# A hybrid scan/attention layer on one Trainium2 core: the scan's queue order around three kinds of short copies

## The chip, the cores and the metric

The kernel runs on one core of one Trainium2 chip. The metric is the device time of one execution in microseconds (us); the time before is the median of three runs. The core has five engines that each work through a queue of their own in order: TensorE (PE in the profile; its weight loads are listed apart as PEld), VectorE (DVE), ScalarE (ACT), GpSimd (POOL) and SyncE (SP). In this kernel SP does nothing but issue DMA transfers, and every transfer is issued there.

## The reference, cut to what matters

One layer of a streaming encoder on 1088 tokens: 1024 of a new prompt and 64 that continue a running stream, with 1024 features. All is fp32.

```
proj = rmsnorm(x) @ w_in          # z | xBC | dt | q | k | v | gate_ssm | gate_att
xs, B, C = silu(causal_conv(xBC)) # 4 groups, each 512 rows of xs and 128 rows of B and of C
per group, over chunks of tokens:
  y      = ((C B^T) * decay) @ (dt * xs) + exp(acum) * (C @ state)
  state  = decay_end * state + B^T @ (to_end * dt * xs)
y_ssm = rmsnorm_per_group((y + D * xs) * silu(z)) * w
o     = diff_attention(q, k, v)
mix   = sigmoid(gate_ssm) * (y_ssm @ w_branch_ssm) + sigmoid(gate_att) * (o @ w_branch_attn)
x    += mix @ w_out
x    += conv_ffn(rmsnorm(x))
```

The prompt starts a group with an empty state; the 64 sample tokens start from a given one. The features of `y_ssm` are 2048, twice those of `o`.

## The kernel before, in words

**Layout.** Activations lie feature by token: 128 features on the partitions, tokens along the row. The 1088 tokens are cut into three column spans `WIDE` of 384, 384 and 320. A large matrix product is made in three terms: each fp32 operand is cast to a rounded type (`hi`) and the difference is kept (`lo`), and `product` (L155 to L160) adds hi*hi, hi*lo and lo*hi over eight slices of 128, 24 matmuls into one bank of PSUM. `acc` (L118) hands the banks out in rotation; in the scan's stage three banks serve, two named `mm` and one named `mx`.

**Order.** The program is traced in Python from top to bottom, and each instruction has the place at which it was traced as its priority. A scheduling pass then writes out one fixed order for each engine. `tc.high_priority(n)` moves what its block traces ahead by n places. `tc.issue_after(ins)` puts what its block traces on the engine of `ins` behind `ins` in that engine's queue; it does not wait for the end of `ins`, and it binds no other engine. What an instruction reads and writes is guarded by semaphores: an instruction at the head of its queue waits for its inputs, and all behind it in that queue wait with it. A tile pool with `bufs=n` has n buffers for a name; the n+1st use waits until the first is no longer read.

**Stages.** Input projections and attention come first, then the scan with what is woven into it, then a third branch product, the output projection and the FFN. The gates are projected by `gate_tiles` (L525), woven into attention and scan, and stored to `g_sc` in DRAM (L533); the branch product reads them from there.

**The scan** (`scan`, L917) goes over 4 groups, each with the three spans, each cut into steps of 128 tokens (the last step of a group has 64): nine steps a group, 36 in all, counted here from 0. Span number `i` runs from 0 to 11, so `i == 6` is the first span of the third group, steps 18, 19 and 20 (`o` = 0, P, 2P). A step has two parts.

- `front` (L826), begun one step ahead: ScalarE makes the exponentials `e2` (L833), TensorE transposes the rows (`tr`, L836) and B (L838) and multiplies B and C into `cb` (L839); ScalarE copies `cb` to `b_cb` (L841); VectorE makes `xx` (L845); GpSimd masks the decay rows `bc` (L846), ScalarE takes their exponentials (L848), VectorE multiplies them by `b_cb` (L849).
- `back` (L852): TensorE makes `yi` (L857) and, with a state, `ye` (L863), which VectorE combines into `y` (L864, L865); at a group's first step there is no state, and ScalarE copies `yi` (L867). TensorE makes the new contribution `stp` (L869). At a group's first step ScalarE copies it to `state` (L872); later GpSimd decays the old state (L874) and VectorE adds (L876). The banks `tr`, `cb`, `yi`, `ye` and `stp` are one each.

At the end of a span follow, in this order:

- `gated` (L881), at the span's last step: VectorE adds D * xs (L883, four), GpSimd multiplies by the gate rows `zin` (L884), ScalarE squares (L885), GpSimd adds the squares in two steps (L886, L887);
- `normed` (L889), in the second step of the next span: TensorE sums over the partitions (`gst`, L891), ScalarE copies to `grs` (L894), and `rstd_of` makes the root;
- `scaled` (L898), in the third step of the next span: VectorE multiplies by the root (L901, four). For groups 0 and 1 ScalarE casts to the hi half in two pieces (L909), written over `zin`, VectorE makes the differences over `y` (L910), and two DMAs store the halves to `y_sc` (L913); for groups 2 and 3 one DMA stores `y` (L904).

The read of the gate rows of the span after (`fetch_z`, L814, `zin`, two buffers) stands behind `scaled` at L952; the rows of a span (`fetch`, L807, buffer `in`, two) are asked for at L959, and the decay rows `bc` (`ask`, L819, four buffers) three steps ahead. The buffers of `y` are two as well (L945).

**What is woven in.** `scan` yields in each step and once more behind a span's `gated`, and at each yield `fill(1.5)` (L593, L986) takes pieces of other work: first the rest of the gate, z and conv projections, then from span `BRANCH_AT` = 4 on the branch products (`branch_tiles`, L974). A piece is one `product` of `branch` (L171): one 128-row block of the output by one span of columns. `branch` asks for its input rows (L178, two calls for each half and span: 12 DMAs), then goes over `TURNS` (L46): the first turn has blocks 0 and 1, so pieces 0 to 5 are (block, span) = (0,0), (1,0), (0,1), (1,1), (0,2), (1,2). For each piece it asks for the gate rows beside it (L192, `b_g`, eight buffers), multiplies, and VectorE empties the bank with the gate, (tanh + 1) * product (L203); a DMA stores the result. The first `branch`, on the attention's `o_sc` with the gates `g_sc[D:]`, is the one that begins in the scan's span 4 (L979); the second (L980) has no gates; the third, after the scan (L1008), has gates and two rows to add.

Of the kernel before, what the change touches and what calls it, by code (L numbers as in the profile page):

```python
# [17 lines left out]
P = 128  # L18
# [45 lines left out]
BRANCH_AT = 4  # L64

# [15 lines left out]
def hybrid_layer(ctx: ExitStack, tc: tile.TileContext, xT, xt, prm, cst, rope, wvd, win, wbs, wba, wout, wup, wdn,  # L81
# [73 lines left out]
    def product(ps, terms):  # L155
        n = len(terms)
        for i, (a_hi, a_lo, b_hi, b_lo) in enumerate(terms):
            PE.matmul(ps, a_hi, b_hi, start=i == 0, stop=False)  # L158
            PE.matmul(ps, a_hi, b_lo, start=False, stop=False)  # L159
            PE.matmul(ps, a_lo, b_hi, start=False, stop=i == n - 1)  # L160
# [9 lines left out]

    def branch(stage, side, src, wts, gates, adds, out, step=1):  # L171

        parts = rows_by_part("b")
        for (c, w), (hi, lo) in zip(WIDE, parts):
            for k in range(0, KT, step):
                if stage is None:
                    for u, t in enumerate((hi, lo)):
                        load(out=t[:, k : k + step].bitcast(F32),  # L178
                             in_=src[D * u + P * k : D * u + P * (k + step), c : c + w].rearrange("(k p) t -> p k t", p=P))
                else:  # L180
                    t = stage()[:, :w]
                    load(out=t, in_=src[P * k : P * (k + 1), c : c + w])
                    S.copy(hi[:, k], t)
                    V.tensor_tensor(out=lo[:, k], in0=t, in1=hi[:, k], op=ALU.subtract)
        for ms in TURNS:
            wt = [weights(wts[m], KT, P) for m in ms]
            for (c, w), (hi, lo) in zip(WIDE, parts):
                for m, (w_hi, w_lo) in zip(ms, wt):
                    beside = []
                    for d, r0 in ([(g_sc, gates)] if gates is not None else []) + [(d, 0) for d in adds]:  # L190
                        t = side()[:, :w]
                        load(out=t, in_=d[r0 + P * m : r0 + P * (m + 1), c : c + w])  # L192
                        beside.append(t)
# [4 lines left out]
                    product(ps, [(w_hi[:, k], w_lo[:, k], hi[:, k], lo[:, k]) for k in range(KT)])  # L198
# [605 lines left out]
    with (tc.tile_pool(name="sin", bufs=1) as sin, tc.tile_pool(name="sp", bufs=1) as sp,  # L804
# [21 lines left out]
        def front(g, ch, o, bx, xs, bc):  # L826
# [14 lines left out]
            S.copy(b_cb[:L, : P + L], cb[:L, : P + L])  # L841
# [10 lines left out]
        def back(g, ch, bx, y, state, start, L, cs, bc, e2, b_cb, xdt, xw):  # L852
# [18 lines left out]
            if state is None:  # L871
                S.copy(new, up)  # L872
            else:
                G.tensor_tensor(out=new.rearrange("p (e q) -> p e q", e=8), in0=state.rearrange("p (e q) -> p e q", e=8),  # L874
                                in1=decs[:, ch, h8].unsqueeze(2).to_broadcast([P, 8, 64]), op=ALU.mult)
                V.tensor_tensor(out=new, in0=new, in1=up, op=ALU.add)  # L876
# [4 lines left out]
        def gated(g, c, w, xs, zt, y):  # L881
            for j in range(4):
                V.scalar_tensor_tensor(y[:, j], xs[:, j, :w], col(O_D + 4 * g + j), y[:, j], ALU.mult, ALU.add)  # L883
            G.tensor_tensor(out=y, in0=y, in1=zt, op=ALU.mult)  # L884
            act(zt, y, AF.Square)  # L885
# [12 lines left out]
        def scaled(g, c, w, xs, zt, y, rs):  # L898
# [3 lines left out]
            if g >= 2:  # L902
                r0 = D * 2 + 4 * P * (g - 2)
                load(out=y_sc[r0 : r0 + 4 * P, c : c + w].rearrange("(j p) t -> p j t", p=P), in_=y)  # L904
                return
# [11 lines left out]
        def scan():  # L917
# [14 lines left out]
            coming = begin(0)  # L932
            for n, (i, g, c, w, o) in enumerate(steps):
                now, coming = coming, begin(n + 1)
# [11 lines left out]
                state = back(g, (c + o) // P, bx, y, state, start, *now)  # L946
                if o == 1 * P and due is not None:
                    rs = normed(*due)
                if o == 2 * P and due is not None:
                    scaled(*due, rs)  # L950
                    if i + 1 < len(spans):
                        gates.append(fetch_z(*spans[i + 1]))  # L952
                if c + o + P >= min(c + w, T):
# [3 lines left out]
                    gated(*due)  # L957
                    if i + 2 < len(spans):
                        got.append(fetch(*spans[i + 2]))  # L959
                    yield i  # L960
            with tc.high_priority(LAST):
                gated(*due)
                scaled(*due, normed(*due))
                for d, t in ends:
# [483 lines left out]
```

## Time and profile before

| | us |
|---|---|
| median of three runs | 2463.59 |
| lowest and highest of them | 2461.98, 2466.84 |
| the profiled execution, as timed | 2464.61 |
| span of its trace | 2462.8 |
| TensorE in the stretch 1050 to 1550 (end of attention, scan): busy | 492.99 of 500 |
| VectorE, ScalarE, GpSimd in the same stretch: busy | 321.74, 267.17, 158.22 |
| DMA share there, and GB/s | 0.69, 236 |
| mean granted TensorE clock there | 0.99 |

Times within the trace count from the start of the span. In rows of a timeline the columns are the start, the duration, the engine, the source line, the operation with out<-in tiles and sizes, and in brackets how long the engine sat idle before it and what ended that. A DMA's row on SP (SPq) is the issue of it, not the transfer. In a table of stretches each engine has its busy time and its count of instructions; a clock of 0.50 is a TensorE that the throttle granted half its rate.

### The profile page before, as it was taken

The numbers are of one execution on the slowest core, as the hardware profiler recorded it, in microseconds if no ns is written. First come the engines' busy times: TensorE is split into PE (matmuls) and PEld (weight loads), VectorE is DVE, ScalarE is ACT, GpSimd is POOL, SyncE is SP. The second block draws the span as 40 slices with busy tenths as digits, with TensorE's granted clock in tenths as the row PEclk, the third lists the DMA queues.
The fourth block names the chain that finished last, engine by engine and source line by source line (L and its number), as shares of the span: only waits on it lengthen the run. The fifth ranks groups of instructions, "written<-read, shape, count | busy, mean of one in ns | idle before, by whom it ended". The sixth has DMA issues, their size and how long they took to land.

```text
span 2462.8 us, 42894 instructions
## 1 busy us (share of the span) xinstructions
PE 2439.4 (99%) x16560; PEld 2363.9 (96%) x16560; DVE 1517.6 (62%) x2574; ACT 1110.8 (45%) x2389; POOL 471.4 (19%) x532
## 2 busy tenths in 40 slices
PE   8999999999999999999999999999999999999999
PEld 8999999999999999998889999999999999999999
DVE  4356266745877577538776664656976677672422
ACT  6244344645665466446664453434544333351200
POOL 0000000100111000005432341012255555530000
PEclk9999999999999999999999999999999999999999
DMA  7237277543444353255697864664222222265542
GB/s 253 91 109 260 93 277 220 160 148 104 151 146 137 119 166 112 89 188 183 227 352 240 304 210 155 221 207 138 68 84 80 80 74 73 79 231 196 188 156 90
DMA packets 221678, 397.61 MB, mean 161 GB/s; under 512 B 31065, under 2 KB 147042, under 8 KB 221346
## 3 DMA queue, kind: packets, MB, share of 16 engines
q1 hardware_dynamic: 221474, 394.88, 48.2%
q8 instruction: 130, 2.13, 0.4%
q14 instruction: 74, 0.61, 0.1%
HBM read 269.03 MB, written 125.76 MB: 160 GB/s over the span
## 4 chain that ended last, share of the span: by engine, by line
PE 88%; DVE 4%; DMA 3%; ACT 1%; issue 1%; POOL 1%; SPq 0%; POOLq 0%; DVEq 0%; ACTq 0%
PE mm L158 13%; PE mm L160 13%; PE mm L159 13%; PE mx L1220 12%; PE mx L160 6%; PE mx L159 6%; PE mx L158 6%; PE mm L1220 5%; PE po L726 3%; PE sc L679 2%; PE sc L678 2%; PE pt L707 1%; PE ye L863 1%; PE yi L857 1%; PE stp L869 1%
## 5 line engine op out<-in xcount | busy, mean ns | idle before, releaser
L158 PE MATMUL mm<-xn_hi,w_hi 128*128 128x384 f32 (+1 forms) x1408 | 471.2, 335 | 1.1 <-DVE zr L542 0.9
L160 PE MATMUL mm<-xn_hi,w_lo 128*128 128x384 f32 (+1 forms) x1408 | 467.8, 332 | 0.5 <-DVE w_lo L152 0.5
L159 PE MATMUL mm<-xn_lo,w_hi 128*128 128x384 f32 (+1 forms) x1408 | 467.1, 332 | 0.0
L151 ACT CAST w_hi<-w_f 128x1024 fp32r<-128x1024 f32 (+2 forms) x137 | 141.8, 1036 | 302.2 <-PE mx L159 184.2
L158 PEld LDWEIGHTS mm<-xn_hi,w_hi 128*128 128x128 f32 x1408 | 264.7, 188 | 6.0 <-DVE zr L542 1.6
L160 PEld LDWEIGHTS mm<-xn_hi,w_lo 128*128 128x128 f32 x1408 | 264.6, 188 | 3.8 <-issue 2.0
L159 PEld LDWEIGHTS mm<-xn_lo,w_hi 128*128 128x128 f32 x1408 | 264.8, 188 | 3.0 <-issue 1.6
L152 DVE TENSOR_TENSOR w_lo<-w_f,w_hi 128x1024 fp32r<-128x1024 f32 (+2 forms) x137 | 169.0, 1234 | 119.0 <-ACT w_hi L151 116.7
L1220 PE MATMUL mx<-n,wh 128*128 128x272 f32 x1128 | 151.5, 290 | 2.6 <-ACT wh L1034 2.6
L158 PE MATMUL mm<-b_hi,w_hi 128*128 128x384 f32 (+1 forms) x448 | 151.3, 338 | 0.7 <-ACT w_hi L151 0.4
L1220 PEld LDWEIGHTS mx<-n,wh 128*128 128x128 f32 x1128 | 146.3, 190 | 2.8 <-ACT wh L1034 2.8
L160 PE MATMUL mm<-b_hi,w_lo 128*128 128x384 f32 (+1 forms) x448 | 147.9, 331 | 0.4 <-DVE w_lo L152 0.4
L159 PE MATMUL mm<-b_lo,w_hi 128*128 128x384 f32 (+1 forms) x448 | 147.7, 330 | 0.1
L692 ACT ACTIVATE p_t<-sc,mx 128x1024 f32<-128x1024 f32 (+5 forms) x144 | 106.2, 740 | 83.0 <-DVE mx L683 41.2
L1220 PE MATMUL mx<-m,w_hi 128*128 128x272 f32 x752 | 142.9, 288 | 0.0
L571 DVE SCALAR_TENSOR_TENSOR cc<-pre,par,cc 128x384 f32<-128x384 f32 (+1 forms) x216 | 125.5, 584 | 16.2 <-ACT cc L569 12.1
L1220 PEld LDWEIGHTS mx<-m,w_hi 128*128 128x128 f32 x752 | 118.1, 188 | 0.0
L1220 PE MATMUL mx<-m,w_lo 128*128 128x272 f32 x376 | 108.3, 288 | 0.0
L1237 POOL TENSOR_TENSOR hb<-hb,cc 128x544 f32<-128x544 f32 (+2 forms) x66 | 85.8, 1314 | 115.1 <-ACT w_hi L1034 88.2
L160 PE MATMUL mx<-xn_hi,w_lo 128*128 128x320 f32 (+1 forms) x320 | 104.1, 326 | 0.1
L158 PE MATMUL mx<-xn_hi,w_hi 128*128 128x320 f32 (+1 forms) x320 | 103.9, 325 | 0.0
L159 PE MATMUL mx<-xn_lo,w_hi 128*128 128x320 f32 (+1 forms) x320 | 103.8, 325 | 0.0
(404 smaller groups left out, 6224.4 us busy)
## 6 DMA issues: line engine op xcount, KB each, us to landing
w_f<-in_win_dram SPq DMA_DIRECT2D x76, 512.0 KB, 4.0
w_f<-in_wup_dram SPq DMA_DIRECT2D x45, 512.0 KB, 3.5
bc<-a_sc SPq DMA_DIRECT2D x32, 512.0 KB, 7.2
xa<-x_sc SPq DMA_DIRECT2D x24, 544.0 KB, 4.8
h_sc<-hb SPq DMA_DIRECT2D x44, 272.0 KB, 2.1
hr<-h_sc SPq DMA_DIRECT2D x22, 544.0 KB, 5.9
x_sc<-cc SPq DMA_DIRECT2D x48, 192.0 KB, 2.4
x_sc<-xa SPq DMA_DIRECT2D x16, 544.0 KB, 2.7
```

Of the source, the lines that this page charges most:

```text
L151: S.copy(hi, w)
L152: V.tensor_tensor(out=lo, in0=w, in1=hi, op=ALU.subtract)
L158: PE.matmul(ps, a_hi, b_hi, start=i == 0, stop=False)
L159: PE.matmul(ps, a_hi, b_lo, start=False, stop=False)
L160: PE.matmul(ps, a_lo, b_hi, start=False, stop=i == n - 1)
L571: V.scalar_tensor_tensor(cc[:, :m], pre[:, i : i + m], cw(i), cc[:, :m], ALU.mult, ALU.add)
L678: PE.matmul(ps[:n, a : a + b], lhs, r_hi, start=True, stop=False)
L679: PE.matmul(ps[:n, a : a + b], lhs, r_lo, start=False, stop=True)
L692: act(p_t[:n, :nk], sc[c][:n, :nk], AF.Exp, bias=mx[:n, c : c + 1], accum_out=dst)
L726: PE.matmul(po[:n, :P], a_t[b // 4][:kw, b % 4 * P : b % 4 * P + n], rhs, start=b == 0, stop=b == nb - 1)
L1220: PE.matmul(ps, w[x][:, c], b[y][:, k], start=start and k == i == 0, stop=k == 3 and i == 2, skip_group_check=not start)
L1237: G.tensor_tensor(out=hb[h][:, o : o + n], in0=hb[h][:, o : o + n], in1=cc[:, d : d + n], op=ALU.mult)
```

## The change

Four things are moved; no arithmetic is added or removed.

1. **Gates ahead of rows.** In the branch that has gates and nothing to add (the attention's), the six gate reads of the first turn are traced ahead of the twelve row reads instead of one ahead of each piece.
2. **Halves.** Casts, differences and stores of the scaled rows leave `scaled` for a new function `halves`. It is traced one step later, in the next span's first step, behind that step's just-begun front, and on ScalarE it stands behind that front's copy of `b_cb` (`issue_after`). The read of gate rows (`fetch_z`) moves there with it, for groups 2 and 3 too.
3. **Squares.** The square and the two sums on GpSimd leave `gated` for a new function `squares`. At a group's last span it is traced after the next group's first step, and on ScalarE it stands behind that step's copy of `state`.
4. **Pieces.** `product` returns its last matmul, and `pieces` keeps those of the branches. At the third group's first span (`i == 6`), on TensorE alone: step 18's back and step 20's front (begun in step 19) stand behind piece 3 (`QUEUED[0]`), step 19's back and the `normed` of span 5 behind piece 5 (`QUEUED[1]`).

```diff
@@ -62,6 +62,7 @@
 ATT_STEPS = 1.66
 SCAN_STEPS = 1.5
 BRANCH_AT = 4
+QUEUED = (3, 5)
 
 
 def group(g):
@@ -157,7 +158,8 @@
         for i, (a_hi, a_lo, b_hi, b_lo) in enumerate(terms):
             PE.matmul(ps, a_hi, b_hi, start=i == 0, stop=False)
             PE.matmul(ps, a_hi, b_lo, start=False, stop=False)
-            PE.matmul(ps, a_lo, b_hi, start=False, stop=i == n - 1)
+            end = PE.matmul(ps, a_lo, b_hi, start=False, stop=i == n - 1)
+        return end
 
     def project(block, evac):
         w_hi, w_lo = weights(block, KT, P)
@@ -168,9 +170,23 @@
                 evac(ps, c, w)
             yield
 
+    pieces = []
+
     def branch(stage, side, src, wts, gates, adds, out, step=1):
 
         parts = rows_by_part("b")
+
+        def next_to(m, c, w):
+            tiles = []
+            for d, r0 in ([(g_sc, gates)] if gates is not None else []) + [(d, 0) for d in adds]:
+                t = side()[:, :w]
+                load(out=t, in_=d[r0 + P * m : r0 + P * (m + 1), c : c + w])
+                tiles.append(t)
+            return tiles
+
+        ready = {}
+        if gates is not None and not adds:
+            ready = {(m, c): next_to(m, c, w) for c, w in WIDE for m in TURNS[0]}
         for (c, w), (hi, lo) in zip(WIDE, parts):
             for k in range(0, KT, step):
                 if stage is None:
@@ -186,16 +202,12 @@
             wt = [weights(wts[m], KT, P) for m in ms]
             for (c, w), (hi, lo) in zip(WIDE, parts):
                 for m, (w_hi, w_lo) in zip(ms, wt):
-                    beside = []
-                    for d, r0 in ([(g_sc, gates)] if gates is not None else []) + [(d, 0) for d in adds]:
-                        t = side()[:, :w]
-                        load(out=t, in_=d[r0 + P * m : r0 + P * (m + 1), c : c + w])
-                        beside.append(t)
+                    beside = ready.pop((m, c)) if (m, c) in ready else next_to(m, c, w)
                     if gates == 0:
                         seen["tanh"] = act(beside[0], beside[0], AF.Tanh, scale=0.5)
                     to = beside[0] if beside else side()[:, :w]
                     ps = acc(w)
-                    product(ps, [(w_hi[:, k], w_lo[:, k], hi[:, k], lo[:, k]) for k in range(KT)])
+                    pieces.append(product(ps, [(w_hi[:, k], w_lo[:, k], hi[:, k], lo[:, k]) for k in range(KT)]))
                     with tc.high_priority(ahead):
                         if not beside:
                             S.copy(to, ps)
@@ -838,7 +850,7 @@
             PE.transpose(cb[:L, 0:P], bx[:, 0, cs], ident)
             PE.matmul(cb[:L, P : P + L], bx[:, 0, cs], bx[:, 1, cs], start=True, stop=True)
             b_cb = sp.tile([P, 2 * P], F32, name="b_cb", tag="b_cb", bufs=3)
-            S.copy(b_cb[:L, : P + L], cb[:L, : P + L])
+            seen["b_cb"] = S.copy(b_cb[:L, : P + L], cb[:L, : P + L])
             xx = sp.tile([P, 2, 8, 64], F32, name="xx", tag="xx", bufs=2)
             xdt, xw = xx[:, 0], xx[:, 1]
             tr3 = tr[:L].rearrange("p (e q) -> p e q", e=8).unsqueeze(1).to_broadcast([L, 2, 8, 64])
@@ -869,7 +881,7 @@
             PE.matmul(up, b_cb[:L, :P], xw[:L].rearrange("p e q -> p (e q)"), start=True, stop=True)
             new = sp.tile([P, 512], F32, name="state", tag="state", bufs=2)
             if state is None:
-                S.copy(new, up)
+                seen["state"] = S.copy(new, up)
             else:
                 G.tensor_tensor(out=new.rearrange("p (e q) -> p e q", e=8), in0=state.rearrange("p (e q) -> p e q", e=8),
                                 in1=decs[:, ch, h8].unsqueeze(2).to_broadcast([P, 8, 64]), op=ALU.mult)
@@ -882,6 +894,8 @@
             for j in range(4):
                 V.scalar_tensor_tensor(y[:, j], xs[:, j, :w], col(O_D + 4 * g + j), y[:, j], ALU.mult, ALU.add)
             G.tensor_tensor(out=y, in0=y, in1=zt, op=ALU.mult)
+
+        def squares(g, c, w, xs, zt, y):
             act(zt, y, AF.Square)
             G.tensor_tensor(out=zt[:, 0:2], in0=zt[:, 0:2], in1=zt[:, 2:4], op=ALU.add)
             G.tensor_tensor(out=zt[:, 0], in0=zt[:, 0], in1=zt[:, 1], op=ALU.add)
@@ -902,6 +916,10 @@
             if g >= 2:
                 r0 = D * 2 + 4 * P * (g - 2)
                 load(out=y_sc[r0 : r0 + 4 * P, c : c + w].rearrange("(j p) t -> p j t", p=P), in_=y)
+
+        def halves(g, c, w, xs, zt, y):
+
+            if g >= 2:
                 return
             hi, lo = zt.bitcast(R32), y.bitcast(R32)
             for j in (0, 2):
@@ -929,9 +947,17 @@
                 i, g, c, w, o = steps[n]
                 return front(g, (c + o) // P, o, *got[i], asked[n])
 
-            coming = begin(0)
+            coming, left, wide = begin(0), None, None
             for n, (i, g, c, w, o) in enumerate(steps):
-                now, coming = coming, begin(n + 1)
+                with ExitStack() as order:
+                    if i == 6 and o == P:
+                        order.enter_context(tc.issue_after(pieces[QUEUED[0]].ins))
+                    now, coming = coming, begin(n + 1)
+                if left is not None:
+                    with tc.issue_after(seen["b_cb"].ins):
+                        halves(*left)
+                    left = None
+                    gates.append(fetch_z(*spans[i]))
                 while ends:
                     d, t = ends.pop()
                     load(out=d, in_=t)
@@ -943,24 +969,36 @@
                 bx, xs = got[i]
                 if o == 0:
                     y = sp.tile([P, 4, 384], F32, name="y", tag="y", bufs=2)
-                state = back(g, (c + o) // P, bx, y, state, start, *now)
-                if o == 1 * P and due is not None:
-                    rs = normed(*due)
+                with ExitStack() as order:
+                    if i == 6 and o < 2 * P:
+                        order.enter_context(tc.issue_after(pieces[QUEUED[o // P]].ins))
+                    state = back(g, (c + o) // P, bx, y, state, start, *now)
+                    if o == 1 * P and due is not None:
+                        rs = normed(*due)
                 if o == 2 * P and due is not None:
                     scaled(*due, rs)
-                    if i + 1 < len(spans):
-                        gates.append(fetch_z(*spans[i + 1]))
+                    left = due if i + 1 < len(spans) else None
+                if wide is not None:
+                    with tc.issue_after(seen["state"].ins):
+                        squares(*wide)
+                    wide = None
                 if c + o + P >= min(c + w, T):
                     due = g, c, w, xs, gates[i], y[:, :, :w]
                     if i + 1 == len(spans):
                         break
                     gated(*due)
+                    if spans[i + 1][0] == g:
+                        squares(*due)
+                    else:
+                        wide = due
                     if i + 2 < len(spans):
                         got.append(fetch(*spans[i + 2]))
                     yield i
             with tc.high_priority(LAST):
                 gated(*due)
+                squares(*due)
                 scaled(*due, normed(*due))
+                halves(*due)
                 for d, t in ends:
                     load(out=d, in_=t)
             yield i
```

## The prediction

> **What bounds it.** I read the head of the page first, then TensorE's waits summed by what ended them, then the granted clock in chosen stretches, then the timeline around the two longest waits of the scan.
>
> ```profile
> span 2462.8 us, 42894 instructions
> PE 2439.4 (99%) x16560; PEld 2363.9 (96%) x16560; DVE 1517.6 (62%) x2574; ACT 1110.8 (45%) x2389; POOL 471.4 (19%) x532
> ```
>
> TensorE (PE) is the bound: 23.4 us of the span are idle, and the change adds or removes no matmul. All it can give lies in TensorE's idle time and in what that does to the clock.
>
> ```profile
> PE ye L863 <- ACT state L872: 3.0, 1, 3.0
> ...
> PE cb L838 <- ACT b_cb L841: 2.0, 1, 2.0
> ```
>
> The columns are the total, the count and the longest. These are the two long waits inside the scan, each a single one, each for a short ScalarE (ACT) copy; the other long ones, for `w_hi` at the kernel's start and `wh` in the FFN, are out of the change's reach. Call the 2.0 us one A, the 3.0 us one B. Right behind each the clock is halved; the columns are the stretch, its length, busy time of PE, PEld, DVE, ACT, POOL, then clock, DMA share and GB/s:
>
> ```profile
> 1157.08:1160.49 3.41, 3.41 (x12) 2.72 (x11) 3.41 (x4) 0.54 (x2) 1.96 (x1) 0.50 0.72 220
> 1283.37:1290.19 6.82, 6.10 (x24) 4.20 (x26) 4.23 (x6) 5.79 (x16) 4.79 (x4) 0.50 0.93 306
> 1240.00:1310.00 70.00, 66.53 (x433) 58.70 (x433) 49.13 (x62) 38.65 (x89) 24.66 (x17) 0.95 1.04 370
> ```
>
> So behind A 3.41 us of matmuls ran at half clock, 3.41/2 = 1.70 us lost; behind B 6.10 us, 3.05 us lost. The third row is the whole stretch around B: DMA is saturated there (share 1.04).
>
> **Halves.** Steps are counted 0 to 35, nine a group; pieces are the branch products, from 0. A, on the timeline:
>
> ```profile
> 1150.29 0.39 PE L839 MATMUL cb<-in 128*128 128x128 f32 x2
> 1151.77 4.40 DVE L901 SCALAR_TENSOR_TENSOR y<-y,par,grs 128x384 f32<-128x384 f32 x4
> 1155.14 0.83 ACT L909 CAST zin<-y 128x768 fp32r<-128x768 f32 x1 [3.92 <-DVE y L901]
> 1155.88 0.37 ACT L841 COPY b_cb<-cb 128x256 f32<-128x256 f32 x1
> 1156.30 0.30 PE L838 MATMUL cb<-con,in 128*64 128x128 f32 x1 [2.04 <-ACT b_cb L841]
> ```
>
> The b_cb copy had its input at 1150.68, but stood in ScalarE's queue behind a cast that waited 3.92 us for VectorE (DVE). The change puts casts behind this copy, so A's 2.04 + 1.70 = 3.74 us go.
>
> What is late next? The casts themselves are not delayed here (they wait for L901 anyway), nor is what hangs on them:
>
> ```profile
> 1160.51 0.37 SPq L913 DMA_DIRECT2D y_sc<-y  x1
> 1165.51 0.69 DVE L864 TENSOR_TENSOR y<-ye,e 128x512 f32<-128x512 f32 x1 [2.69 <-DMA y_sc<-y]
> 1179.27 2.38 DVE L910 TENSOR_TENSOR y<-y,zin 128x768 fp32r<-128x768 f32 x2
> 1183.03 1.93 DVE L883 SCALAR_TENSOR_TENSOR y<-in,par,y 128x320 f32<-128x320 f32 x4
> 1184.98 0.33 SPq L810 DMA_DIRECT2D in<-x_sc  x1
> 1194.04 0.63 PE L836 MATMUL tr<-con,in 128*128 128x128 f32 x4 [0.80 <-DMA in<-x_sc]
> ```
>
> VectorE waits for the store of the scaled rows until 1165.51 whatever TensorE does; its later work ends in L883, which frees the `in` buffer; the next rows are asked for at 1184.98, and TensorE waits for them until 1194.04. A TensorE that is 3.74 us ahead meets the same rows. It keeps only what VectorE gives: the two L910 differences (2.38 us) stand before L883 now and come after it in traced order then. Kept: 0 to 2.38 us, less 1.70 us if the longer wait at 1194 halves the clock as A did. I take 1.2, the middle, since the advance is spent in several waits from L864 on.
>
> The halves move past one front and past the z read, which moves with them. For the six spans of groups 0 and 1 two casts, two differences and two stores of up to 768 KB come later, on ScalarE's, VectorE's and SP's queue; for ten spans the z read comes one step later. That read I cost at nothing: here it was asked for at 1245.63 and used at 1279.37 (L884, below), 33.7 us later, and a step is 8 us (`yi` of step 16 to `yi` of step 18, 1261.11 to 1277.48, halved). With that cover gone L884 and the squares behind it would be late, not TensorE directly.
>
> The stores free the `y` buffer for the span after next. Where the halves really move, the new wait is on L864, with L876, L865 and L845 queued behind it on VectorE, and TensorE's `yi` bank behind L865 (the last row is from the DMA view of 1225 to 1310: count, KB each, median us to landing):
>
> ```profile
> 1245.63 0.73 SPq L816 DMA_DIRECT2D zin<-z_sc  x1
> 1246.04 0.37 ACT L841 COPY b_cb<-cb 128x256 f32<-128x256 f32 x1 [0.29 <-PE cb L839]
> 1246.85 2.97 DVE L849 TENSOR_TENSOR bc<-bc,b_cb 128x1024 f32<-128x1024 f32 x1
> 1255.19 0.69 DVE L864 TENSOR_TENSOR y<-ye,e 128x512 f32<-128x512 f32 x1
> 1261.11 1.09 PE L857 MATMUL yi<-bc,xx 128*64 128x128 f32 x16
> y_sc<-zin SPq DMA_DIRECT2D x2, 768.0 KB, 9.5
> ```
>
> At step 15: two casts from 1246.41 end at 1248.07, the two differences after L849 at 1249.82 + 1.82 = 1251.6, the store lands 9.5 us later at 1261.1. L864, L876 and L865 (0.69 + 0.69 + 0.68) end at 1263.2, so `yi` at 1261.11 waits 2.1 us, with a halved window 3.8. Lower end 0: the row at 1165.51 is the same wait, 2.69 us on VectorE, and TensorE had no gap from it. That is the nearest row; I take 0.
>
> **Squares, pieces, gates.** B:
>
> ```profile
> 1278.51 1.12 PE L869 MATMUL stp<-xx,b_cb 128*128 128x512 f32 x2
> 1279.37 2.90 POOL L884 TENSOR_TENSOR y<-y,zin 128x1280 f32<-128x1280 f32 x1 [2.15 <-DVE y L883]
> 1280.47 0.66 PE L836 MATMUL tr<-con,in 128*128 128x128 f32 x4 [0.50 <-DVE xx L845]
> 1282.30 1.27 ACT L885 ACTIVATE zin<-y 128x1280 f32<-128x1280 f32 x1 [0.44 <-POOL y L884]
> 1283.47 0.57 ACT L872 COPY state<-stp 128x512 f32<-128x512 f32 x1
> 1284.09 2.08 PE L863 MATMUL ye<-in,state 128*128 128x128 f32 x8 [2.97 <-ACT state L872]
> ```
>
> Step 18's state copy stood behind the square L885, and that behind GpSimd's product. Without the square it could start where ScalarE fell idle, at 1282.30 - 0.44 = 1281.9, so the squares alone give some 1.6 us of B. The rest comes from the pieces: TensorE went from step 18 to 19 with nothing between, since pieces 3 to 5 stood behind both steps (rows of three engines, and three of that DMA view):
>
> ```profile
> 1264.26 1.70 SPq L533 DMA_DIRECT2D g_sc<-gt  x1
> 1266.49 0.42 SPq L178 DMA_DIRECT2D b_lo<-o_sc  x1
> 1276.47 2.94 SPq L192 DMA_DIRECT2D b_g<-g_sc  x4
> b_g<-g_sc SPq DMA_DIRECT2D x9, 192.0 KB, 8.4
> g_sc<-gt SPq DMA_DIRECT2D x4, 192.0 KB, 8.0
> b_lo<-o_sc SPq DMA_DIRECT2D x2, 640.0 KB, 10.5
> 1287.95 1.01 DVE L203 SCALAR_TENSOR_TENSOR b_g<-b_g,mm 128x384 f32<-128x384 f32 x2
> 1277.48 1.09 PE L857 MATMUL yi<-bc,xx 128*64 128x128 f32 x16
> 1290.52 0.44 PE L158 MATMUL mm<-b_hi,w_hi 128*128 128x384 f32 x1
> 1294.82 0.31 PE L158 MATMUL mm<-b_hi,w_hi 128*128 128x320 f32 x1
> ```
>
> Three accumulators serve the pieces, so piece 3 needs piece 0's bank, and that is emptied (L203) only with its gate, asked for at 1276.47, landing 8.4 us later at 1284.9. With gates there by 1277.5, piece 3 (4.30 us) runs ahead of step 18's `yi`, pieces 4 and 5 (320 wide, so 320/384 of that, 3.6 us each) ahead of step 19's `ye`. The state copy then hides beneath 7.2 us of pieces; even in B, with the square ahead of it, it was done 4.4 us after `stp` (1279.63 to 1284.04). The 0.50 us before `tr` goes too. The later square with its two sums on GpSimd is awaited only by step 19's `gst`, which stands behind the same pieces, so I cost it at nothing; without them it would be up to its own 1.27 us and two sums late. All of TensorE is now queued behind pieces 3 and 5. B gives 0.50 + 2.97 + 3.05 = 6.52 us.
>
> The six gates, 1088 KB, take 3.0 us of DMA at 370 GB/s. If all of it falls ahead of the rows, the last row part lands at 1266.49 + 10.5 + 3.0 = 1280.0, and piece 4 wants it at 1277.48 + 4.30 = 1281.8: hidden, with 1.8 us to spare, 0.6 with the 1.2 us of A. I take 0.
>
> **Sum.** 6.52 + 1.2 = 7.7 us. The profiled execution took 2464.61 us (span 2462.8 and 1.8 around it), 1.0 over the median of 2463.59, so 2456.9 for it and 2455.9 for the median.
>
> **A rule weighed.** A's gap of 2.04 us halved the clock, the 0.80 us gap at 1194 did not (no halved stretch stands behind it). The Trainium skill, "TensorE: Matmul & The Clock Gate", Part 1, says the clock halves after at least one idle window of about 3.4 us, in windows that run free of the kernel. By that A's 1.70 us would not be owed to A, and the rival "A kept whole" would come out 1.7 us later. The row decides for me: half clock followed a gap of 2.04.
>
> **Rivals.** *A kept whole*: VectorE's queue shifts with TensorE and nothing waits at 1194. For it: VectorE idles 2.69 us before 1165.51; against: that is for a store that does not move. Gain 6.52 + 3.74 = 10.3, 2453.3 us. Chance 0.18.
>
> *The y buffer*: the store behind the later halves holds L864 at step 15. For it: 9.5 us landings; against: no gap from the 2.69 us wait. Gain 7.7 - 3.8 = 3.9, 2459.7 us. Chance 0.22.
>
> *Gates not ready*: the gate reads head SP's queue, but cannot go before the last `g_sc` store has landed, 1264.26 + 8.0 = 1272.3; in the profile they do come only after it, which speaks for this. Rows and weights queue behind them, and TensorE, now bound to run piece 3 first, stands at 1277.5. With row reads of 1259 to 1266 put off by up to 8 us, piece 4 waits to about 1290: 8 to 12 us idle and 3 us of half clock against the 6.52 removed, so 5 to 9 us lost less A's 1.2. It decides from a gate landing after about 1281. Against: the rows of g_sc that these six read are from the first gate blocks, written far earlier in traced order. 2469.5 us, chance 0.14.
>
> That the order edges bind nothing is no rival: in A and B the rows stand in the opposite order.
>
> **Chances.** Forecast 0.46. A measurement of this kernel can tell about 0.2%, 4.9 us, from no change, so below 2458.7 is faster: the forecast and *A kept whole*, less the forecast's edge (A at -1.7), 0.62. The y buffer and edges are within, 0.25. Slower 0.13. The range runs from *A kept whole* with A's following 0.80 us gap gone as well, 2452, to both bad bounds at once, 6.52 - 1.7 - 3.8 = 1.0 gained, 2462.6, with a little of *gates not ready*: 2464.
>
> **What would show it.** Right: no TensorE wait for b_cb or state over 0.5 us, no 0.50 clock in 1150 to 1300, b_g reads before 1270, pieces 3 to 5 around `yi` and `ye` of step 18 and 19, the `in` wait near 1194 at 1 to 3 us. Wrong: a new halved stretch in the scan, L864 or L867 waiting for `y_sc<-y`, or PE idle before piece 3.

## The result and the profile after

The change made the kernel a little slower: the median of 20 runs is 2467.95 us (2465.67 to 2472.78) against 2464.80 us (2461.26 to 2467.28) for 20 runs of the kernel before, ratio 1.0016 with a 95% interval of 1.0010 to 1.0022 (the ratios here are estimates from all runs of both kernels, not quotients of the two medians). The forecast was 2455.9 with a range that ended at 2464. The profiled execution took 2467.65 us, its span is 2465.8. The scan's lines 836 to 883 stand 12 further down (841 is now 853, 849 is 861, 864 is 876, 872 is 884, 876 is 888), 887, 891 and 901 are 901, 905 and 915, and 158, 192, 203, 533 and 1220 are 159, 183, 215, 545 and 1258.

The head of the page after, and TensorE's waits summed by what ended them:

```profile
span 2465.8 us, 42904 instructions
PE 2436.2 (99%) x16560; PEld 2362.0 (96%) x16560; DVE 1526.4 (62%) x2574; ACT 1111.7 (45%) x2389; POOL 474.5 (19%) x532
```

```profile
PE mm L159 <- DVE b_g L215: 6.5, 1, 6.5
PE mx L159 <- ACT w_hi L335: 6.4, 2, 5.9
PE mx L1258 <- ACT wh L1072: 2.6, 1, 2.6
PE mx L1258 <- DVE u L1285: 1.6, 1, 1.6
PE stp L881 <- DVE state L888: 1.5, 1, 1.5
PE mx L1258 <- ACT m L1072: 1.1, 1, 1.1
...
PE yi L869 <- DVE y L877: 0.8, 1, 0.8
...
PE cb L850 <- ACT b_cb L853: 0.5, 1, 0.5
```

The columns of the waits are the total, the count and the longest. TensorE is busy 3.2 us less (less half clock) and idle 6.2 us more. The two waits of before are gone: `ye` no longer waits for `state`, and the wait for `b_cb` is 0.5 us. In their place stands one of 6.5 us for `b_g`, some small ones for VectorE, and two in the FFN, a stage that the diff does not touch. The timeline of the changed kernel around the long one:

```profile
1266.34 1.50 SPq L545 DMA_DIRECT2D g_sc<-gt  x1
...
1275.22 6.31 SPq L183 DMA_DIRECT2D b_g<-g_sc  x6
...
1278.11 0.66 PE L848 MATMUL tr<-con,in 128*128 128x128 f32 x4
...
1283.53 1.22 DVE L861 TENSOR_TENSOR bc<-bc,b_cb 128x1024 f32<-128x1024 f32 x1
1284.66 1.01 DVE L215 SCALAR_TENSOR_TENSOR b_g<-b_g,mm 128x384 f32<-128x384 f32 x2
...
1285.26 0.69 PE L159 MATMUL mm<-b_hi,w_hi 128*128 128x384 f32 x1 [6.50 <-DVE b_g L215]
```

The six gate reads, though traced ahead of the rows, are issued at 1275.22, behind the last store of a gate tile, 1.25 us earlier than in the kernel before. The first of them takes 8.4 us to land, at 1283.6. VectorE, which has no idle time from 1267.83 on, comes to the emptying of the bank at 1284.66, and piece 3 starts at 1285.26. So the gate accounts for the wait up to 1283.6, and the last 1.05 us before the emptying are VectorE's queue. In the kernel before the first gate landed later still (1276.47 + 10.1 = 1286.6) and its bank was emptied at 1287.95, but TensorE went on with steps 18 and 19 meanwhile. Now their backs stand behind the pieces. The stretch of half clock behind the gap (columns as in the prediction):

```profile
1282.08:1288.91 6.83, 3.65 (x11) 3.65 (x12) 4.06 (x6) 1.57 (x4) 6.48 (x2) 0.50 0.95 282
```

That is 3.65/2 = 1.82 us lost on top of the gap. The sums by stage are in the next table. For A (1145 to 1240), B (1240 to 1320) and the end of the scan (1525 to 1570; each counted with the scan's start at 1073.5) they are TensorE's idle time plus half its busy time at half clock, the FFN's is its length from its first `mx<-n,wh` matmul to the end of TensorE's last. "Order" names kernels in which the FFN's TensorE instructions stand in the same order. Each ratio is to runs of the kernel before made beside that kernel, whose medians went from 2464.03 to 2464.80, so medians of different rows compare to within that.

| kernel | median, us | ratio to before | A | B | end | FFN | order |
|---|---|---|---|---|---|---|---|
| before | 2464.80 | 1 | 4.55 | 6.52 | 1.25 | 728.32 | a |
| after | 2467.95 | 1.0016 (1.0010 to 1.0022) | 3.96 | 8.32 | 1.27 | 729.84 | b |
| e1, no queued pieces | 2465.75 | 1.0006 (0.9997 to 1.0015) | 3.79 | 6.08 | 2.49 | 728.36 | a |
| e2, gt pool kept | 2464.66 | 1.0004 (0.9995 to 1.0012) | 4.71 | 0.00 | 6.18 | 729.30 | d |
| e3, halves as before | 2473.32 | 1.0035 (1.0023 to 1.0048) | 5.19 | 12.02 | 1.46 | 730.74 | c |
| e4, only halves | 2465.65 | 1.0004 (0.9996 to 1.0013) | 3.68 | 5.93 | 1.75 | 728.33 | a |
| e5, after, two pools | 2457.24 | 0.9973 (0.9962 to 0.9983) | 3.83 | 0.00 | 1.71 | 728.25 | a |
| e6, before, two pools | 2457.48 | 0.9976 (0.9965 to 0.9987) | 4.79 | 0.00 | 1.88 | 728.22 | a |
| e7, only squares | 2466.05 | 1.0008 (0.9999 to 1.0017) | 4.08 | 5.99 | 1.92 | 730.60 | c |
| e8, two pools, halves as before | 2457.78 | 0.9974 (0.9964 to 0.9984) | 3.94 | 0.00 | 1.08 | 728.37 | a |
| e9, rows first | 2468.95 | 1.0015 (1.0006 to 1.0024) | 4.47 | 8.09 | 1.21 | 729.90 | b |
| e10, scratch of their own | 2468.14 | 1.0014 (1.0005 to 1.0023) | 4.08 | 9.55 | 1.03 | 729.86 | b |
| e11, squares as before | 2468.62 | 1.0014 (1.0005 to 1.0023) | 4.30 | 9.36 | 1.66 | 729.88 | b |

So of the 3.0 us between the two spans, B brings 8.32 - 6.52 = +1.8, A 3.96 - 4.55 = -0.6, the FFN +1.5. The scan's start is 0.66 us later, in a part that the change leaves alone; over the 13 profiles it lies between 1072.65 and 1076.08. That makes 3.4; the 0.4 us too many were not traced to a place.

### The profile page after: what moved, and what is told of

It is laid out like the page before. It is cut to its first block, busy times and chain, and to the rows that moved or that the text cites. A ratio compares the mean times of both kernels' runs of the same rounds, so it can differ in the third digit from the quotient of the medians.

```text
span 2465.8 us, 42904 instructions
## 1 busy us (share of the span) xinstructions
PE 2436.2 (99%) x16560; PEld 2362.0 (96%) x16560; DVE 1526.4 (62%) x2574; ACT 1111.7 (45%) x2389; POOL 474.5 (19%) x532
## 4 chain that ended last, share of the span: by engine, by line
PE 88%; DVE 4%; DMA 4%; ACT 1%; issue 1%; POOL 1%; SPq 1%; DVEq 0%; POOLq 0%; ACTq 0%
PE mm L159 13%; PE mm L161 13%; PE mm L160 13%; PE mx L1258 12%; PE mx L161 7%; PE mx L160 6%; PE mx L159 6%; PE mm L1258 5%; PE po L738 3%; PE sc L691 2%; PE sc L690 2%; PE pt L719 1%; PE yi L869 1%; PE ye L875 1%; PE stp L881 1%
```

## The experiments

Theory G: the loss is the wait for the gates, since the order edges put TensorE's scan behind a piece that needs them; and the gates are late not for their place in a queue or for DRAM but for their space in SBUF. The kernel frees two pools and takes one in their place (L976 to L978 of before):

```
cv_pool.release()        # pre, cc of the conv tiles
st.release()             # gt, zr: three of 1536 bytes a partition
bs = tc.alloc_tile_pool(name="bs", bufs=1, side="right")   # b_f (three), b_g (eight)
```

Theory H, the rival: the later halves cost it, through the store of the halves and VectorE. Theory F came with the profile after: a moved scan moves the order of the FFN's instructions too.

**e1**, the changed kernel without its order edges.

```diff
-                    if i == 6 and o == P:
-                        order.enter_context(tc.issue_after(pieces[QUEUED[0]].ins))
...
-                    if i == 6 and o < 2 * P:
-                        order.enter_context(tc.issue_after(pieces[QUEUED[o // P]].ins))
```

> The changed kernel without its fourth part (TensorE's scan steps are no longer queued behind pieces 3 and 5); gates ahead of rows, halves and squares stay. Theory G (the 6.50 us that TensorE waits before piece 3, and the half clock behind it, are the loss: step 18's back stands in TensorE's queue behind a piece whose bank is emptied only once the first gate row is there): the wait for b_g before a piece goes, the pieces are late but hidden again, and of B the part that the square made is gone, so some 1.0 to 1.5 us for the state copy stay, perhaps with a half clock window: span 2465.8 - 6.5 - 1.8 + 1.3 + 1.7 = 2460.5, or 2459 if the FFN's instructions stand as before too (its two new waits of 1.14 and 1.62 us less a half clock window of 1.7); ratio to before 0.998 to 0.999. Rival H (the halves cost it: small waits for y and state in 1155 to 1230 and the store of the later halves): the time stays within 1 us of the changed kernel's 2467.95.

TensorE's longest waits in e1 from 1145 to 1320:

```profile
PE mm L159 <- DVE b_g L215: 3.2, 1, 3.2
PE stp L881 <- DVE state L888: 1.4, 1, 1.4
PE ye L875 <- ACT state L884: 1.2, 1, 1.2
```

The wait for `b_g` shrinks to 3.2 us, it does not go; the state copy still costs 1.2. The median is 2.2 us below the changed kernel's, and 1.5 of that is the FFN, back in order a. The span, 2465.5, is not G's 2459 to 2460.5, and the median is not within H's 1 us of the changed kernel's. What is left of the wait is not the gate: the first one lands 8.4 us after 1276.56, at 1285.0, but VectorE works without idle time from 1280.22 and comes to the emptying 3.8 us later:

```profile
1286.08 2.78 DVE L861 TENSOR_TENSOR bc<-bc,b_cb 128x1024 f32<-128x1024 f32 x1
1288.79 1.00 DVE L215 SCALAR_TENSOR_TENSOR b_g<-b_g,mm 128x384 f32<-128x384 f32 x2
```

So piece 3 had two bounds, the late gates and, close behind, the place of the emptying in VectorE's fixed order. G named the first alone.

**e2**, the pool of `gt` kept to the end of the branches, so that `b_g` takes over the conv tiles' space alone; `b_f` had to move to the scan's space.

```diff
             cv_pool.release()
-            st.release()
...
+    bf = tc.alloc_tile_pool(name="bf", bufs=1, side="right")
     run(branch(stage, side, y_sc[2 * D :], wbs[1], 0, (n_sc, m_sc), mixed))
```

> The changed kernel, with the pool of the staged gt tiles kept to the end of the branches, so that the gate buffers b_g no longer lie in a pool that takes over its space (the third branch's staging tiles get a pool of their own after the scan). Theory G, in its form that the gate reads wait for the space: they are issued some 90 us earlier, right behind the last conv tiles, the 6.50 us wait before piece 3 is gone and with it the half clock behind it (3.65 us of matmuls at half rate, 1.8 us): span 2465.8 - 8.3 = 2457.5, the chain of pieces 3 to 5 before or around step 18 and 19, ratio 0.997. Rival D (the gates come late because SP's queue and the DMA engines are full from 1240 to 1310): reads still land after 1275, a wait of 3 to 6 us before piece 3 stays, 2462 to 2466. Rival H: the small waits between 1155 and 1230 stay in either case and the time is no better than 2464.

B is 0.00: the gates come with the conv tiles' end and TensorE has no wait in 1240 to 1320. So it was the space, and rival D fell. But 4.9 us come back at the scan's end: the third branch's first three rows, read 285 us after the scan's start in the kernel before, are read at 439, since their tiles wait for the scan's pools. The median is 3.3 us below the changed kernel's, not 8.3. A, B and the end together fall by 2.7 us and the FFN by 0.5, but from the scan's first transposition to the FFN the profile is only 0.8 us shorter: some 1.9 us of the matmuls' own time came on top, which stays unexplained. (From before to e6 the same sums fall by 5.7 us and the stretch by 6.8, so they are good to 1 or 2 us.)

**e5 and e6**, the clean form: the pool is cut in two at the same addresses. `b_f`, three tiles of 1536 bytes, takes exactly the space of the three `gt` and `zr` tiles, `b_g` the rest. e5 does it to the changed kernel, e6 to the kernel before, with nothing else.

```diff
-            bs = tc.alloc_tile_pool(name="bs", bufs=1, side="right")
+            bf = tc.alloc_tile_pool(name="bf", bufs=1, side="right")
+            bs = tc.alloc_tile_pool(name="bs", bufs=1, side="right")
...
-            return bs.tile([P, 384], F32, name="b_f", tag="b_f", bufs=BF)
+            return bf.tile([P, 384], F32, name="b_f", tag="b_f", bufs=BF)
```

> The changed kernel with the branches' pool cut in two at the same addresses: the three staging tiles b_f take over exactly the space of the gt tiles, the eight gate buffers b_g the space of the conv tiles beyond it, so that a gate read waits only for the conv tiles' readers. (In the run with the gt pool kept, the b_f tiles had to lie in the scan's space, so the third branch's first rows came later.) Theory G (the space of b_g is what the gates waited for): the gates are read before 1200, no wait before piece 3, no half clock in 1240 to 1320, and the FFN's instructions stand as in the kernel before, so its stage takes 719.1 us as there: span 2462.8 - 6.5 (B) - 0.6 (A net) = 2455.7, ratio 0.997. Rival E (the scan's end is pinned by the third branch's rows, which come through three staging buffers): 4 to 5 of these 7 us come back as waits for b_hi in 1525 to 1570, as 4.47 + 1.71 us did with the gt pool kept: 2460, ratio 0.9985 to 0.9995.

> The kernel before with the branches' pool cut in two at the same addresses and nothing else: no gates ahead of rows, no later halves, no later squares, no queued pieces. Theory G: the pieces' gates come early, the pieces run ahead of step 18 by themselves, B's 3.47 us of waits and 3.05 us of half clock go, A's 2.04 + 1.70 stay: span 2462.8 - 6.5 = 2456.3, ratio 0.9975. Rival Q (the order edges and the later squares are needed for that): B's wait for state stays at 1.5 us or more, 2460 to 2463. Rival E: 4 to 5 us of the gain come back in 1525 to 1570, 2461.

The gate reads in e5 and in e6, two stretches of e6 (1145 to 1240, 1240 to 1320), and the emptying of the banks of pieces 0, 1 and 2 in e5:

```profile
1093.97 3.78 SPq L183 DMA_DIRECT2D b_g<-g_sc  x8
```

```profile
1094.88 3.74 SPq L183 DMA_DIRECT2D b_g<-g_sc  x8
```

```profile
1145.00:1240.00 95.00, 91.92 (x631) 81.71 (x630) 72.00 (x86) 61.11 (x144) 40.59 (x25) 0.98 0.69 222
1240.00:1320.00 80.00, 80.00 (x544) 72.99 (x543) 60.10 (x75) 44.56 (x102) 31.34 (x20) 1.00 0.97 348
```

```profile
1260.60 0.56 DVE L215 SCALAR_TENSOR_TENSOR b_g<-b_g,mm 128x384 f32<-128x384 f32 x1 [2.58 <-PE mm L161]
1269.30 0.54 DVE L215 SCALAR_TENSOR_TENSOR b_g<-b_g,mm 128x384 f32<-128x384 f32 x1
1274.31 0.54 DVE L215 SCALAR_TENSOR_TENSOR b_g<-b_g,mx 128x384 f32<-128x384 f32 x1
```

The reads are issued 181 us earlier and TensorE is busy 80.00 of 80.00 us at full clock. Both kernels gain about 7 us (e5 2457.24, e6 2457.48; before, beside them, 2464.45). Rivals Q and E fell: no order edge, no later square is needed, and little comes back at the end (1.71 and 1.88 us for 1.27 and 1.25). The cut alone gives about what the change was forecast to give, and the change's four parts on top of it add nothing that the intervals tell apart. The cut also changed VectorE's order: the three emptyings stand apart, each soon after its piece, where the changed kernel has them together from 1284.66. No run separates early gates from that order; both came with the pool.

**e10 and e9** take the other two explanations of the late gates: the DRAM tensor they share with the last stores, and their place behind the rows.

```diff
-                load(out=g_sc[P * j : P * (j + 1), c : c + w], in_=gt)
+                load(out=(g_sc if j < KT else ga_sc)[P * (j % KT) : P * (j % KT + 1), c : c + w], in_=gt)
```

```diff
-        if gates is not None and not adds:
+        if False:
             ready = {(m, c): next_to(m, c, w) for c, w in WIDE for m in TURNS[0]}
```

> The changed kernel with the attention's gates in a scratch tensor of their own in DRAM, so that the gate reads share nothing in DRAM with the last stores of the other gates; the pools are the changed kernel's. Theory G (it is the space in SBUF): nothing changes, the wait of 6 to 7 us before piece 3 and the FFN's 729.8 us stay, 2466 to 2469, ratio 1.001 to 1.002. Rival D2 (the reads wait for the stores into the same DRAM tensor): the gates come 80 us earlier and the time is that of the run with two pools, 2457, ratio 0.997.

> The changed kernel without its first part: the gate reads of the first turn stand behind the row reads again, one ahead of each piece. TensorE's order is the changed kernel's, instruction by instruction. Theory G (all gate reads wait for the space of the gt tiles, whatever stands ahead of what on SP's queue): the reads move by 1 to 2 us at most, the wait before piece 3 stays at 6.5 to 8.5 us with its half clock: span 2465.8 to 2468, ratio to before 1.001 to 1.002; the FFN's stage, 729.8 us in the changed kernel with the same order, is 729.8 again. By the forecast on record, which gave this part the pieces' readiness, the wait would be several us longer than in the changed kernel.

SP's issues in e10, and TensorE's longest wait there from 1145 to 1320:

```profile
1266.88 1.50 SPq L545 DMA_DIRECT2D g_sc<-gt  x1
1275.74 6.32 SPq L183 DMA_DIRECT2D b_g<-ga_sc  x6
```

```profile
PE mm L159 <- DVE b_g L215: 7.1, 1, 7.1
```

With a tensor of their own the reads still stand behind the last `g_sc<-gt`. Without the first part the wait is 6.5 us, as with it. Theory G in its last form (the reads wait for the space) holds, and part 1 of the change did nothing that can be measured.

**e3, e8 and e4** ask what the halves are worth: with late gates (e3 against the changed kernel), with gates in time (e8 against e5), and alone (e4). In e3 and e8 the casts, differences, stores and the gate-row read stand behind `scaled` again.

```diff
-                    left = due if i + 1 < len(spans) else None
+                    halves(*due)
+                    if i + 1 < len(spans):
+                        gates.append(fetch_z(*spans[i + 1]))
```

> The changed kernel with the casts, differences, stores and gate-row reads of the halves where they were before; gates ahead of rows, squares and queued pieces stay. Theory G: the wait for b_g before piece 3 stays at 5 to 7 us with half clock behind it, A comes back with 2.04 us and its half clock window of 1.7 us, the small waits of 1155 to 1230 (4.0 us in all) go: 2465.8 + 3.7 - 4.0 = 2465.5, ratio 1.001. Rival H: at least 2.5 us faster than the changed kernel, 2465 or less by the timer.

> The changed kernel with the branches' pool cut in two, and with the halves and gate-row reads where they were before; against the run that has the later halves too, it shows what they are worth when the gates are in time. Theory G with A's sum as the runs so far have it (2.84 + 1.71 us of idle and half clock in 1145 to 1240 before, 3.7 to 4.7 with later halves): within 1 us of the run with later halves, 2456 to 2457. Rival A (A kept whole, 3.7 us): 3 us or more slower than it, 2459.

> The kernel before with the second part of the change alone: the halves and the gate-row reads one step later. Theory G: A's 2.04 us and its half clock (1.7 us) go, small waits of some 4.0 us for state, y and cb come in 1155 to 1230 and 0.8 us before tr goes, B stays at 2.97 us with its half clock: within 1 us of before, ratio 0.9995 to 1.0003. Rival H: VectorE waits for the later stores and hands the delay on to TensorE: 2 to 4 us slower than before, ratio 1.001. By the forecast on record it would be 1.2 us faster.

TensorE's waits in e3 from 1145 to 1320, SP's issue of its gate reads, and VectorE's emptying of the first bank:

```profile
PE mm L159 <- DVE b_g L215: 9.9, 1, 9.9
PE tr L848 <- DMA in<-x_sc: 2.1, 1, 2.1
PE cb L850 <- ACT b_cb L853: 1.4, 1, 1.4
```

```profile
1278.09 6.22 SPq L183 DMA_DIRECT2D b_g<-g_sc  x6
```

```profile
1288.46 1.02 DVE L215 SCALAR_TENSOR_TENSOR b_g<-b_g,mm 128x384 f32<-128x384 f32 x2 [3.54 <-DMA b_g<-g_sc]
```

H fell as the cause of the loss, and G's number for e3 too: two stores of halves and a `bc` read stand ahead of the gates again, the gates go out 2.9 us later, and the wait grows to 9.9 us. Here VectorE itself idles 3.54 us for the gate, so the gate alone sets the wait. In the changed kernel the later halves softened the loss; what is left of H is VectorE's 1.05 us there. With gates in time they are worth nothing (e8 and e5 differ by 0.5 us in the median), and alone nothing that can be told from no change (e4, 1.0004). In e4 B is 5.93 us, near G's sum but not by the wait that G named: 3.0 us are for `b_g`, whose first gate landed at 1283.7 and was used by VectorE at 1287.38, and 1.4 for `state`.

**e7 and e11** ask the same of the squares: alone, and taken from the changed kernel.

```diff
-                    if spans[i + 1][0] == g:
-                        squares(*due)
-                    else:
-                        wide = due
+                    squares(*due)
```

> The kernel before with the third part of the change alone: the square and its two sums at a group's last span stand behind the next group's first copy of state. Theory F (whatever moves in the scan also moves where the FFN's first instructions stand, and that costs there): the FFN's order here is that of the run with halves as before, whose stage took 721.5 us instead of 719.1; B's wait for state falls from 2.97 to some 1.4 us with one half clock window less (1.5 us): 2462.8 - 1.6 - 1.5 + 2.4 = 2462.1, ratio 0.9995 to 1.0. Without theory F: 2459.7, ratio 0.9985.

> The changed kernel without its third part: the square and its sums at a group's last span stand where they were. Theory G: the wait before piece 3 rules B whatever ScalarE does, so nothing moves: B's sum 8.3 us, the FFN's stage 729.8 us with the same order, ratio 1.001 to 1.002. By the forecast on record the squares were worth 1.6 us of B: 1 to 2 us slower than the changed kernel.

Two of TensorE's waits in e7 from 1145 to 1320:

```profile
PE ye L875 <- ACT state L884: 1.4, 1, 1.4
PE gst L905 <- POOL zin L901: 1.4, 1, 1.4
```

In e7 the state copy is awaited 1.4 us instead of 3.0, the 1.6 that the prediction gave the squares. But `gst` now waits 1.4 us for the later sums on GpSimd, and the FFN takes 2.3 us more. Theory F held for the FFN (2.4 us expected, and e3's order), but not for the total, a span of 2464.8 us for 2462.1: with `gst`'s wait and its half clock B stayed at 5.99. (The 719.1 and 721.5 us in the expectations of e5 and e7 are the FFN counted over a shorter stretch than the table's.) In e11 the wait is 6.5 us as in the changed kernel, and B's 9.36 differs from its 8.32 by half clock alone.

**The FFN.** Its first and last matmuls, before, after and e7:

```profile
L1220 PE MATMUL mx<-n,wh x1128: 282/288/428, 1731.1 to 2187.5; 128*128 128x272 f32 x188
```

```profile
L1258 PE MATMUL mx<-n,wh x1128: 283/288/396, 1732.6 to 2190.5; 128*128 128x272 f32 x188
```

```profile
L1251 PE MATMUL mx<-n,wh x1128: 283/288/428, 1730.7 to 2189.4; 128*128 128x272 f32 x188
```

From first to last of these matmuls it is 456.4, 457.9 and 458.7 us. The scheduling pass gave the FFN's first pairs four different orders in the 13 kernels. Six kernels with order a lie within 0.15 us of each other, whatever their scan did; b, c and d cost 1.5, 2.3 and 1.0 us. Four of the six have a window of half clock in the FFN, 3.41 us long, and e5 and e6 have none: there the half clock does not show in the length. That the order is the cause is a reading of 13 profiles: no run put another order behind the same scan, and what tips the pass was not tried.

## Why the prediction was wrong

- **What bounds it**: right. Nearly all gain and loss is TensorE's idle time and its half clock, with the FFN's, unforeseen, among it.
- **Gates**, the step that failed: "With gates there by 1277.5, piece 3 (4.30 us) runs ahead of step 18's `yi`", with the six reads at 0 cost. The first was there at 1283.6, and its bank was empty for piece 3 at 1285.26; "PE idle before piece 3", the prediction's own sign of being wrong, was 6.50 us. Even in the kernel before the row was misread: 8.4 us is the median of nine reads, the first took 10.1, and the emptying stood in VectorE's queue until 1287.95. The rival *gates not ready* named the wait for the last `g_sc` store and was argued down because the rows read had been written long before. That is true of the rows (e10), but it was the buffer that had to wait, and I looked for the source's dependencies and not for the destination's. The rival's way to the loss was another, piece 4 waiting for rows, and its price was too high: it put 5 to 9 us lost for B, and B lost 1.8 (8.32 in place of 6.52). That its 2469.5 us is the nearest of the times named to the measured 2467.95 is partly luck: the FFN's 1.5 and the later start's 0.7 us, which it did not name, are in the measured time.
- **Pieces**: the edges took the cover from the late gates. Where the gates come in time (e5, e6) pieces 3 to 5 all run ahead of step 18, in e6 without an edge, and B is 0.00, as the sum of 6.52 said. The state copy hides beneath the piece behind step 18 (1290.88 to 1295.13 in e5), not beneath 4 and 5 as forecast.
- **Squares**: 1.6 us of the wait, as worked out. The later sums cost nothing behind the pieces, as said (no wait for `gst` in the changed kernel), and 1.4 us where no piece covers `gst` (e7), which the prediction had allowed for in words.
- **A**: 0.6 us measured (3.96 against 4.55) for the 1.2 forecast, but not by the wait near 1194 that was named. In the changed kernel it is VectorE:

```profile
1152.83 4.40 DVE L915 SCALAR_TENSOR_TENSOR y<-y,par,grs 128x384 f32<-128x384 f32 x4
1157.16 1.21 DVE L861 TENSOR_TENSOR bc<-bc,b_cb 128x1024 f32<-128x1024 f32 x1
1158.29 0.67 DVE L888 TENSOR_TENSOR state<-state,stp 128x512 f32<-128x512 f32 x1
...
1159.02 1.13 PE L881 MATMUL stp<-xx,b_cb 128*128 128x512 f32 x2 [1.47 <-DVE state L888]
...
1267.83 0.69 DVE L876 TENSOR_TENSOR y<-ye,e 128x512 f32<-128x512 f32 x1 [3.82 <-DMA y_sc<-y]
```

  The cast had waited for the four scalings; freed of the cast, TensorE waits for the state sum that stands behind the same four on VectorE, since `stp` has one bank. What held the queue was itself held, and what else it holds is next.
- **The y buffer**: the wait came where it was placed, at step 15 and with 3.82 us, on VectorE alone. The store was later than worked out: the two differences took 3.47 us there, not 1.82, and it landed at 1267.7, not 1261.1. TensorE had pieces then, so 0 was right at that place. But from this wait VectorE worked without idle time up to the emptying at 1284.66, so up to 1.05 us of the 6.50 can be owed to it; no run shows how much.
- **The FFN**: no step looked beyond the scan; 1.5 us of the 3.0 between the spans.

## What to carry to other kernels

Before an order is written by hand so that one thing covers another, ask when each input of the cover is ready, and for a transfer ask both ends: the source's writers, and the last readers of whatever lay in the destination's space, pool by pool, and whether the engine that must use the transfer is free when it lands. A wait that an edge should hide may go for nothing when one pool is cut in two. In a kernel whose order is fixed ahead as a whole, compare the order of the stages that the edit does not touch: an edit worth a few us can lose as much there.

## What the runs showed of the hardware

The clock halves by windows of a fixed grid, not by the length of a gap. In the kernel before the halved stretches begin at 1157.08, 1283.37 and 1744.17: 37 and 135 times 3.413 us apart. The same wait for `b_cb` fell into one window in e6 and across two in e8 (stretches of one window each; columns as above):

```profile
1154.10:1157.51 3.41, 1.39 (x9) 1.20 (x10) 3.41 (x6) 2.48 (x5) 0.42 (x1) 1.00 0.00 0
1157.51:1160.93 3.42, 3.42 (x10) 2.38 (x9) 3.42 (x3) 0.00 (x0) 1.96 (x1) 0.50 0.91 296
```

```profile
1152.11:1155.52 3.41, 2.38 (x24) 1.70 (x22) 3.41 (x3) 0.07 (x1) 2.81 (x2) 1.00 0.14 48
1155.52:1158.94 3.42, 2.33 (x13) 1.92 (x14) 3.42 (x5) 2.41 (x5) 0.92 (x1) 1.00 0.18 66
1158.94:1162.35 3.41, 3.41 (x20) 2.90 (x19) 3.41 (x4) 0.52 (x2) 1.04 (x1) 1.00 1.01 295
```

With 2.02 us idle in one window the next is halved; with 2.12 us split into 1.03 and 1.09 none is. Over 13 profiles, the last 10 us of each left out, 21 of 22 full-clock windows with 1.73 us idle or more were followed by a halved one, and of those with 0.8 to 1.65 us one was, with 1.25. The Trainium skill, "TensorE: Matmul & The Clock Gate", Part 1, has the free-running window of about 3.4 us, and the traces agree; it asks for an idle window, and here about half a window idle was enough. So the 1.70 us behind A was owed to A by its place in the grid, and can be won or lost by a shift of 1 us.
